# Moving high-part splits to ScalarE, and gate weights and compression weights ahead, in a hybrid decoder layer

## The chip, the cores and the metric

The kernel runs on one core of a Trainium2 chip, as one program. The metric is device microseconds of one execution. The engines are named as in the profile: PE is TensorE's matmuls, PEld its weight loads, DVE is VectorE, ACT is ScalarE, POOL is GpSimd, and SP is the engine that issues nearly all DMAs.

## What is computed

One decoder layer on 512 tokens of width 1024, in float32: a recurrent branch (RG-LRU, width 1344 in four blocks of 336) and native sparse attention (16 heads, 4 key/value groups) share one input projection, are merged by gates, and a squared-ReLU MLP follows. Cut to what the change touches:

```python
xn = rmsnorm(x, norm_mix)
(u_rnn, u_gate, q, k_c, v_c, k_s, v_s, k_w, v_w, g_nsa, g_a, g_b) = jnp.split(xn @ w_in, cuts, axis=-1)
h_a = rg_lru(causal_depthwise_conv(u_rnn, conv_w, conv_b), gate_a_w, gate_a_b, gate_x_w, gate_x_b, lru_lambda)
y_a = h_a * jax.nn.gelu(u_gate, approximate=True)
y_b = nsa_mixer(q, k_c, v_c, k_s, v_s, k_w, v_w, g_nsa, ...)
merged = jax.nn.sigmoid(g_a) * (y_a @ proj_a) + jax.nn.sigmoid(g_b) * (y_b @ proj_b)
h = x + merged @ w_out
return h + jnp.square(jax.nn.relu(rmsnorm(h, norm_mlp) @ w_mlp_in)) @ w_mlp_out
# rg_lru, per block of 336: r, i = sigmoid(block_diag(u)); a = exp(c * r);
# h_t = a_t h_{t-1} + sqrt(1 - a_t^2) (i_t u_t)
# nsa_mixer: rmsnorm over 64 for q, k_s, k_w; k_c, v_c go through compress_blocks (w1, gelu, w2)
```

## The kernel before

**Split precision.** Every matrix product is three matmuls (`mm3`, lines 142 to 144). An operand is cut into a rounded high part (`wh`, line 135 or 137) and a low part, the operand minus its high part (`wl`, line 138, always on VectorE); the product is high times high, high times low, low times high. `split` does this for weights: its flag `act` puts the high part on ScalarE, else it is on POOL. Prepared activations have pairs too: `XH`/`XL` (normed input), `uh`/`ul` (recurrent input, lines 361 and 362), `YH`/`YL` (recurrent output, lines 398 and 399). A tile's first high-times-low matmul can't start before the low part is written, and the low part waits for the high part.

**Order.** The code is written against a tile framework whose scheduler puts the instructions of each engine in one fixed order; `high_priority` pulls splits ahead, `keep_in_program_order` and `issue_after` pin instructions. On the chip each engine runs its list in order and waits where an operand or a buffer is not ready. SP issues the DMAs in such a list too, and stands still where the next one waits.

**Stages, in the profile's microseconds.** Up to 30 the input is normed and transposed. From 30 to 204 stands the recurrent branch: 21 tiles of 128 features (`u_tiles`, 24 matmuls of 512 columns each; tile n has `mm` as its PSUM buffer) and, between them, four recurrent blocks `lru(b)`. A u tile's weights come two tiles at a time (`wraw`, 1 MB, two buffers) and are split (`wh`, `wl`, two buffers each). Its sink is a convolution (`uc`, lines 332 and 334) that a DMA regroups into `ub`, or a gelu (`gs`, `gg`, lines 322 to 325). A block `lru(b)` takes its gate weights (`graw`, two DMAs of 441 KB), splits them (`gwh`, `gwl`), multiplies, and runs a chain over its three parts: tanh (line 375), exp and tanh (376, 377), VectorE's `rr` (379), `ee` = 1 - a (380, POOL), `rr` again (381), `ii` (382), one square root for all three (383), and a scan (387) whose result `y_tile` multiplies by the gelu and splits. The square root and the tanh family need different function tables.

From 204 to 266 four token-major projections of keys and values (`tok_cols`: KS, VS, KW, VW) and the first queries (Q) follow, each in pieces of weights, each with four accumulators of 128 tokens; keys and queries are normed per head (`head_norm`, one tile of 128 tokens at a time, with `rstd_heads`). From 266 to 345 the compression (`ZW` projections, then `phi` with its weights `praw` and `w2r`, split into `pwh`, `pwl`, `w2h`) runs with part of another projection as filler. Then attention to 620, the merge to 725, and the MLP.

The lines the change touches: `split` (126 to 139), `prep` (166), `lru` (356 to 392), `y_tile` (394), `u_tiles` and the calls behind it (400 to 475), `tok_cols` (511), `head_norm` (528), and the sequence of the token-major calls and the compression's loads (617 to 645). The functions follow with the profile's line numbers.

Of the kernel before, what the change touches and what calls it, by code (L numbers as in the profile page):

```python
# [45 lines left out]
GT = 1  # L46
# [23 lines left out]
def layer(ctx, tc, x, norm_mix, w_in, conv_w, conv_b, gate_a_w, gate_a_b, gate_x_w, gate_x_b,  # L70
# [78 lines left out]
    class Cols:  # L149
# [205 lines left out]

    def lru(b):
# [6 lines left out]
        wts = [split(v, 3, BLK, rn, ("gwh", "gwl")) for v in GR.pop(b)]  # L363
# [4 lines left out]
        for j in range(3):  # L368
# [11 lines left out]
            G.tensor_scalar(E[:, j], R[:, j], -1.0, 1.0, op0=OP.mult, op1=OP.add)  # L380
# [13 lines left out]
    def y_tile(t):  # L394
# [80 lines left out]
    for t in (0, 8, 9, 10):  # L475
        y_tile(t)
# [33 lines left out]

    def tok_cols(c0, n, sink):
        step = WH // n
        pss = [psr.tile([128, T], F32, name="lru", bufs=4) for _ in range(4)]
        per = 8 if 8 * n <= WR else 4
        for k0 in [k for c in range(0, 8, per) for k in range(c, c + per, step)]:
            if k0 % per == 0:
                v = raw(128, per, n, (None, rows(win, c0, n)[:, k0:k0 + per]))
            kr = k0 % per
            k1 = min(kr + step, per) - kr + k0
            wh, wl = split(v[:, kr:kr + k1 - k0], k1 - k0, n)  # L520
            for i in range(4):
                ts = slice(128 * i, 128 * i + 128)
                for k in range(k0, k1):
                    mm3(pss[i][:, :n], XH[:, k, ts], XL[:, k, ts], wh[:, k - k0], wl[:, k - k0], k == 0, k == 7)
# [3 lines left out]
    def head_norm(d4, ps, pl):  # L528
# [27 lines left out]
    def q_sink(i, ps):  # L556
        head_norm(QN[0][:, i].rearrange("p (h d) -> p h d", d=64), ps, kvp)
# [59 lines left out]
    with pool("kvp") as kvp:  # L617
# [3 lines left out]
        tok_cols(COL_VW, 304, v_sink(1))  # L621
        for h in range(BC):
            bias_copies(h)
        tok_cols(COL_Q, 256, q_sink)
    with pool("ph") as ph:
# [628 lines left out]
```

## Time and profile before

| what | us |
|---|---|
| runs: median of 3 (lowest to highest) | 1067.66 (1067.63 to 1069.73) |
| the profiled execution, its own time | 1072.21 |
| its span in the trace | 1070.5 |
| PE busy in the span | 1039.5 (97%) |
| DVE, ACT, POOL busy | 664.6, 360.6, 361.4 |

TensorE's mean granted clock in the profiled execution is 0.995. PE is busy in nearly every slice of the span, so what can be won or lost lies in the stretches where it waits or where its clock is lower: the rows below give these one by one. A number in brackets behind an instruction is the idle time just before it on its engine and what ended it.

### The profile page before, as it was taken

The page shows a single profiled execution, that of the slowest core. Times are in us where ns is not written, and L with a number is a line of the kernel's source. Part 1 is how long each engine was busy: PE and PEld are TensorE (multiplying, and loading weights), DVE is VectorE, ACT ScalarE, POOL GpSimd, SP SyncE. Part 2 cuts the span into 40 slices and gives each one's busy share as a digit, 9 for nine tenths or more (in the row PEclk, how much of TensorE's full clock was granted, in tenths as well). Part 3 has the DMA queues.
Part 4 walks back from the last instruction along what each step waited for, and adds up shares of the span by engine and source line. Part 5 has one row for each costly group of instructions (what it writes and reads, how often), then busy time and mean ns, then how long its engine had stood idle before and what let it go on. Part 6 is the DMA issues. An engine that isn't in the chain of part 4 may idle for free.

```text
span 1070.5 us, 14779 instructions
## 1 busy us (share of the span) xinstructions
PE 1039.5 (97%) x5405; PEld 882.1 (82%) x5405; DVE 664.6 (62%) x1227; ACT 360.6 (34%) x770; POOL 361.4 (34%) x397
## 2 busy tenths in 40 slices
PE   6989899999999999999999999999999999999998
PEld 5757676899778898988988888888888888888887
DVE  5579889964675787768778659554333343444443
ACT  4142542522333476756757631032111111111110
POOL 4233344353232464655645433202111121111110
PEclk9989999999999999999999999999999999999999
DMA  7625324243554634424333267512232323322322
GB/s 179 152 83 159 104 75 129 81 125 119 138 156 121 203 93 128 139 81 122 99 122 110 80 226 282 203 46 79 79 118 79 117 80 118 101 97 87 110 79 79
DMA packets 110039, 127.89 MB, mean 119 GB/s; under 512 B 23087, under 2 KB 87375, under 8 KB 109967
## 3 DMA queue, kind: packets, MB, share of 16 engines
q1 hardware_dynamic: 109967, 126.94, 39.2%
q8 instruction: 43, 0.70, 0.3%
q14 instruction: 29, 0.24, 0.1%
HBM read 109.45 MB, written 15.64 MB: 117 GB/s over the span
## 4 chain that ended last, share of the span: by engine, by line
PE 78%; DVE 9%; DMA 6%; issue 4%; POOL 1%; ACT 1%; SPq 0%; DVEq 0%; POOLq 0%; ACTq 0%
PE mf L142 6%; PE mf L143 6%; PE mf L144 6%; PE am L144 5%; PE am L143 5%; PE am L142 5%; PE mi L144 5%; PE mi L142 5%; PE mi L143 5%; PE sc L886 4%; PE po L924 3%; PE pt L905 3%; PE lru L143 3%; PE lru L144 3%; PE lru L142 3%
## 5 line engine op out<-in xcount | busy, mean ns | idle before, releaser
L137 POOL TENSOR_SCALAR wh<-wraw 128x1024 fp32r<-128x1024 f32 (+2 forms) x103 | 110.7, 1075 | 246.5 <-PE mi L143 119.2
L138 DVE TENSOR_TENSOR wl<-wraw,wh 128x1024 fp32r<-128x1024 f32 (+2 forms) x111 | 133.3, 1202 | 54.8 <-POOL wh L137 45.6
L897 POOL TENSOR_SCALAR pp<-pp,sm,gates 128x512 f32<-128x512 f32 (+3 forms) x128 | 93.9, 741 | 67.7 <-DVE sm L895 45.0
L143 PE MATMUL am<-mwl,zh 128*128 128x512 f32 x256 | 99.3, 389 | 0.0
L144 PE MATMUL am<-mwh,zl 128*128 128x512 f32 x256 | 99.3, 389 | 0.0
L142 PE MATMUL am<-mwh,zh 128*128 128x512 f32 x256 | 98.8, 389 | 0.0
L144 PE MATMUL mi<-XH,wl 128*128 128x512 f32 x240 | 93.5, 390 | 0.3 <-DVE wl L138 0.3
L142 PE MATMUL mi<-XH,wh 128*128 128x512 f32 x240 | 93.5, 389 | 0.1
L143 PE MATMUL mi<-XL,wh 128*128 128x512 f32 x240 | 93.4, 389 | 0.0
L1197 DVE TENSOR_TENSOR zl<-Z,zh 128x512 fp32r<-128x512 f32 x32 | 36.3, 1136 | 88.4 <-ACT zh L1196 88.4
L144 PE MATMUL mm<-XH,wl 128*128 128x512 f32 (+1 forms) x216 | 82.4, 383 | 5.5 <-DVE wl L138 5.5
L142 PE MATMUL mm<-XH,wh 128*128 128x512 f32 (+1 forms) x216 | 82.6, 384 | 0.7 <-DVE uc L334 0.6
L143 PE MATMUL mm<-XL,wh 128*128 128x512 f32 (+1 forms) x216 | 82.3, 382 | 1.0 <-DVE XL L225 1.0
L894 ACT ACTIVATE pp<-pp,mx 128x512 f32<-128x512 f32 (+3 forms) x128 | 71.5, 561 | 29.4 <-DVE mx L892 26.6
L1170 DVE SCALAR_TENSOR_TENSOR Z<-mi,zr 128x512 f32<-128x512 f32 x30 | 20.7, 691 | 96.9 <-ACT zr L1169 96.9
L137 POOL TENSOR_SCALAR mwh<-wraw 128x1024 fp32r<-128x1024 f32 x32 | 34.1, 1067 | 138.2 <-PE am L144 131.0
L892 DVE CUSTOM_DVE_ANT_0 pp<-sc,BT 128x512 f32<-128x512 f32 (+3 forms) x128 | 59.0, 484 | 15.1 <-PE pt L905 7.3
L1196 ACT ACTIVATE zh<-Z 128x512 fp32r<-128x512 f32 x32 | 20.3, 633 | 136.5 <-PE am L143 134.4
L1169 ACT ACTIVATE zr<-mi 128x512 f32<-128x512 f32 x30 | 18.0, 600 | 141.7 <-PE mi L144 136.9
L911 ACT ACTIVATE PH<-pt 128x512 fp32r<-128x512 f32 (+1 forms) x96 | 49.3, 524 | 33.9 <-PE pt L905 33.3
L912 DVE TENSOR_TENSOR PL<-pt,PH 128x512 fp32r<-128x512 f32 (+1 forms) x96 | 56.0, 592 | 5.8 <-ACT PH L911 5.6
L886 PE MATMUL sc<-KK,QS 128*128 128x512 f32 (+3 forms) x256 | 57.8, 334 | 0.0
(294 smaller groups left out, 2698.6 us busy)
## 6 DMA issues: line engine op xcount, KB each, us to landing
wraw<-in_w_in_dram SPq DMA_DIRECT2D x26, 1024.0 KB, 5.3
wraw<-in_w_mlp_in_dram SPq DMA_DIRECT2D x16, 1024.0 KB, 5.6
wraw<-in_w_mlp_out_dram SPq DMA_DIRECT2D x16, 1024.0 KB, 4.8
tab_p<-tab_t SPq DMA_DIRECT2D x16, 320.0 KB, 5.0
wraw<-in_proj_a_dram SPq DMA_DIRECT2D x8, 640.0 KB, 5.4
BT<-tab_p SPq DMA_DIRECT2D x16, 256.0 KB, 2.7
wraw<-in_proj_b_dram SPq DMA_DIRECT2D x4, 1024.0 KB, 5.4
wraw<-in_w_out_dram SPq DMA_DIRECT2D x4, 1024.0 KB, 5.6
```

The costliest lines, as they stand in the source:

```text
L137: G.tensor_scalar(h, v, 1.0, 0.0, op0=OP.mult, op1=OP.add)
L138: V.tensor_tensor(l, v, f32(h), op=OP.subtract)
L142: PE.matmul(ps, lh, rh, start=start, stop=False)
L143: PE.matmul(ps, lh, rl, start=False, stop=False)
L144: return PE.matmul(ps, ll, rh, start=False, stop=stop)
L886: ins = PE.matmul(ps[:, cs], grp.Q[r][:, ts], grp.K[br][:, hl, :128 * (i + 1)], start=hl == 0, stop=hl == 1)
L892: V.tensor_tensor_reduce(out=pp[:, cs], in0=ps[:, cs], in1=BTS[h][:, 384 - 128 * i:], scale=1.0, scalar=3e38, op0=OP.add, op1=OP.min, accu ...
L894: S.activation(pp[:, cs], pp[:, cs], AF.Exp, bias=mx, scale=-1.0, accum_out=sm)
L897: G.tensor_scalar(pp[:, cs], pp[:, cs], sm, gt, op0=OP.mult, op1=OP.mult)
L911: S.activation(ph, pv, AF.Copy)
L912: V.tensor_tensor(pl, pv, f32(ph), op=OP.subtract)
L1197: V.tensor_tensor(zl, Z[:, f], f32(zh), op=OP.subtract)
```

## The change

Five edits go together.

1. **Splits on ScalarE.** The high parts of the u tiles 2 to 20 (19 of them) are made by ScalarE, not POOL; the `ee` of the recurrent blocks (12) too, as `Copy` with scale and bias; and the `YH` of the y tiles 1 to 7 (the last call's four stay on POOL). `uh` and `gwh` stay on POOL.
2. **First gate weights early.** `load_gates(0)` is called before the u tiles' sinks, and the gate weights of the first block are split behind the split of tile 5, before `lru(0)` is issued.
3. **Norms of four tiles at once.** `head_norm` copies and squares each of its four tiles and makes the reciprocal roots of all sixteen heads in one go; the query norms of the attention stage keep the old form under the name `row_norm`.
4. **Compression early.** The pool of the compression opens before the token-major calls, and its weights' DMAs and first splits are issued between KW and VW.
5. **Token-major pieces in turn.** VW (304 columns) is loaded as 6 and 2 rows of 128 instead of 4 and 4, in three pieces (3, 3, 2 rows) instead of four (3, 1, 3, 1), and `issue_after` keeps the matmuls of one piece behind those of the piece before.

```diff
-            V.tensor_tensor(l, v, f32(h), op=OP.subtract)
+            split_last[0] = V.tensor_tensor(l, v, f32(h), op=OP.subtract).ins
...
-        def prep(self, n, prio=PRIO):
+        def prep(self, n, prio=PRIO, act=False):
...
+                self.got[n] = split(self.load(n), 8, 128, prio=prio, act=act or self.act, **own)
...
+    def split_gates(b):
+        if b not in GW3:
+            GW3[b] = [split(v, 3, BLK, rn, ("gwh", "gwl")) for v in GR.pop(b)]
...
-        wts = [split(v, 3, BLK, rn, ("gwh", "gwl")) for v in GR.pop(b)]
+        split_gates(b)
+        wts = GW3.pop(b)
         load_gates(b + 1)
...
-            G.tensor_scalar(E[:, j], R[:, j], -1.0, 1.0, op0=OP.mult, op1=OP.add)
+            S.activation(E[:, j], R[:, j], AF.Copy, bias=1.0, scale=-1.0)
...
-        G.tensor_scalar(YH[p:, t], y, 1.0, 0.0, op0=OP.mult, op1=OP.add)
+        if act:
+            S.activation(YH[p:, t], y, AF.Copy)
+        else:
+            G.tensor_scalar(YH[p:, t], y, 1.0, 0.0, op0=OP.mult, op1=OP.add)
...
-            UW.prep(n + 1)
+            UW.prep(n + 1, act=n >= 2)
...
+    load_gates(0)
+    UW.prep(2, act=True)
     for n in range(2):
         u_sink(UO[n])(p2[n])
-    u_tiles(2, 2 + GT)
-    load_gates(0)
-    u_tiles(2 + GT, 6)
+    u_tiles(2, 5)
+    with tc.issue_after(split_last[0]):
+        split_gates(0)
+    u_tiles(5, 6)
...
-        per = 8 if 8 * n <= WR else 4
-        for k0 in [k for c in range(0, 8, per) for k in range(c, c + per, step)]:
+        per = min(8, WR // n // step * step)
+        for k0 in range(0, 8, step):
...
+                if tok_last:
+                    es.enter_context(tc.issue_after(tok_last[-1]))
...
+    def head_norm(d, i, ps, pl, key):
...
+        S.activation(d[:, i], src, AF.Copy)
+        S.activation(SQ[key][:, i], ps[:, :256], AF.Square)
+        if i == 3:
+            rs = rstd_heads(SQ.pop(key).rearrange("p i (h d) -> p (i h) d", d=64), 16, "hrs", pl)
+            rv = rs.rearrange("p (i h) -> p i h", h=4)
+            for n in range(4):
+                V.tensor_tensor(d[:, n], d[:, n], rv[:, n].unsqueeze(2).to_broadcast([128, 4, 64]), op=OP.mult)
...
-    with pool("kvp") as kvp:
+    with pool("ph") as ph:
         tok_cols(COL_KS, 256, k_sink(0))
         tok_cols(COL_VS, 256, v_sink(0))
         tok_cols(COL_KW, 256, k_sink(1))
-        tok_cols(COL_VW, 304, v_sink(1))
-        for h in range(BC):
-            bias_copies(h)
-        tok_cols(COL_Q, 256, q_sink)
-    with pool("ph") as ph:
...
+        tok_cols(COL_VW, 304, v_sink(1))
+        for h in range(BC):
+            bias_copies(h)
+        tok_cols(COL_Q, 256, q_sink)
```

Where it moves instructions, at three places. The first is SP's list at the first u tiles, about 31 to 49 us: the end of the small constants (`pek`, `pev`), the weights of tiles 4 and 5 (`wraw_419`), the regrouping of the convolution (`ub` from `uc`) and the gate weights of the first block (`graw`). Before:

```order
L286 DMA pev_345<-in_phi_v_pe_dram 64x16x1 x2
L122 DMA wraw_419<-in_w_in_dram 128x8x256
L122 DMA wraw_492<-in_w_in_dram 128x8x256
L340 DMA ub_364<-uc_359 112x512
L340 DMA ub_364<-uc_359 16x512
L340 DMA ub_364<-uc_367 96x512
L340 DMA ub_364<-uc_367 32x512
L340 DMA ub_364<-uc_407 80x512
L340 DMA ub_413<-uc_407 48x512
L122 DMA graw_415<-in_gate_a_w_dram 112x3x336
L122 DMA graw_417<-in_gate_x_w_dram 112x3x336
```

and now:

```order
L287 DMA pev_345<-in_phi_v_pe_dram 64x16x1 x2
L121 DMA graw_359<-in_gate_a_w_dram 112x3x336
L121 DMA graw_361<-in_gate_x_w_dram 112x3x336
L121 DMA wraw_419<-in_w_in_dram 128x8x256
L121 DMA wraw_500<-in_w_in_dram 128x8x256
L341 DMA ub_372<-uc_367 112x512
L341 DMA ub_372<-uc_367 16x512
L341 DMA ub_372<-uc_375 96x512
L341 DMA ub_372<-uc_375 32x512
```

Both `graw` loads went from behind the `ub` transfers to just ahead of the weights of tiles 4 and 5.

The second place is POOL at the same tiles: `wh_374`, `wh_378`, `wh_421`, `wh_457`, `wh_494`, `wh_710` are the high parts of the tiles 2 to 7, `gwh` the gate weights' and `uh` the recurrent input's. Before:

```order
L137 TENSOR_SCALAR wh_374<-wraw_284 128x1024
L137 TENSOR_SCALAR wh_378<-wraw_284 128x1024
L137 TENSOR_SCALAR wh_421<-wraw_419 128x1024
L361 TENSOR_SCALAR uh_571<-ub_364 112x512 x2
L137 TENSOR_SCALAR wh_457<-wraw_419 128x1024
L361 TENSOR_SCALAR uh_571<-ub_364 112x512
L455 MEMSET wraw_696 16x128
L460 MEMSET wraw_696 16x16x33
L137 TENSOR_SCALAR gwh_579<-graw_415 112x1008
L137 TENSOR_SCALAR wh_494<-wraw_492 128x1024
L137 TENSOR_SCALAR gwh_583<-graw_417 112x1008
L137 TENSOR_SCALAR wh_710<-wraw_492 128x1024
```

Now POOL has

```order
L138 TENSOR_SCALAR gwh_492<-graw_359 112x1008
L138 TENSOR_SCALAR gwh_496<-graw_361 112x1008
L368 TENSOR_SCALAR uh_579<-ub_372 112x512 x3
L469 MEMSET wraw_696 16x128
L474 MEMSET wraw_696 16x16x33
L368 TENSOR_SCALAR uh_863<-ub_417 112x512
L138 TENSOR_SCALAR gwh_871<-graw_587 112x1008
L138 TENSOR_SCALAR gwh_875<-graw_589 112x1008
```

and the tiles' high parts (`wh_363`, `wh_382`, `wh_421`, `wh_457`) stand on ScalarE among the convolutions' first steps:

```order
L136 ACTIVATE wh_363<-wraw_284 128x1024
L333 ACTIVATE uc_367<-mm_106,cb_311,cw_310 128x512
L136 ACTIVATE wh_382<-wraw_284 128x1024
L333 ACTIVATE uc_375<-mm_107,cb_311,cw_310 128x512
L136 ACTIVATE wh_421<-wraw_419 128x1024
L333 ACTIVATE uc_411<-mm_386,cb_311,cw_310 128x512
L136 ACTIVATE wh_457<-wraw_419 128x1024
```

POOL keeps the gate weights and `uh`, and the gate weights are now first in its list; the tiles' splits went to ScalarE.

The third place is VectorE before tile 10's low part (`wl_1023`), inside the second recurrent block. Before:

```order
L138 TENSOR_TENSOR gwl_1146<-graw_879,gwh_1145 112x1008
L379 SCALAR_TENSOR_TENSOR rr_883<-ee_884,rr_883 112x512
L138 TENSOR_TENSOR gwl_1150<-graw_881,gwh_1149 112x1008
L382 SCALAR_TENSOR_TENSOR ii_885<-ii_885,ub_413 112x512
L381 SCALAR_TENSOR_TENSOR rr_883<-rr_883 112x512
L334 SCALAR_TENSOR_TENSOR uc_1013<-mm_988,cw_310,uc_1013 128x511
L138 TENSOR_TENSOR wl_1023<-wraw_1020,wh_1022 128x1024
L334 SCALAR_TENSOR_TENSOR uc_1013<-mm_988,cw_310,uc_1013 128x510
```

and now:

```order
L139 TENSOR_TENSOR gwl_1146<-graw_879,gwh_1145 112x1008
L387 SCALAR_TENSOR_TENSOR rr_883<-ee_884,rr_883 112x512
L139 TENSOR_TENSOR gwl_1150<-graw_881,gwh_1149 112x1008
L390 SCALAR_TENSOR_TENSOR ii_885<-ii_885,ub_417 112x512
L139 TENSOR_TENSOR wl_1023<-wraw_1020,wh_1022 128x1024
L335 SCALAR_TENSOR_TENSOR uc_1013<-mm_988,cw_310,uc_1013 128x511
L389 SCALAR_TENSOR_TENSOR rr_883<-rr_883 112x512
L335 SCALAR_TENSOR_TENSOR uc_1013<-mm_988,cw_310,uc_1013 128x510
```

Ahead of `wl_1023` the last `rr` of line 381 (now 389) and one step of the convolution went behind it; the two `gwl` and the `ii` stay ahead.

## Rows read from the trace of the kernel before

**Rows 1.** Waits of PE over the span: total us, times, longest us.

```profile
PE mm L144 <- DVE wl L138: 5.5, 4, 3.0
PE lru L144 <- DVE gwl L138: 2.3, 1, 2.3
PE lru L143 <- DVE wl L138: 1.7, 2, 1.5
PE lru L142 <- POOL uh L361: 1.4, 2, 0.9
PE lru L142 <- POOL gwh L137: 1.2, 1, 1.2
...
PE mm L142 <- DVE uc L334: 0.6, 1, 0.6
```

**Rows 2.** Windows: us, busy (count) of PE, PEld, DVE, ACT, POOL, then PEclk, DMA, GB/s.

```profile
130.00:210.00 80.00, 77.72 (x360) 61.82 (x358) 73.01 (x88) 35.77 (x47) 32.13 (x29) 1.00 0.31 94
352.00:620.00 268.00, 268.00 (x1691) 240.45 (x1690) 205.25 (x636) 170.77 (x449) 141.19 (x182) 1.00 0.39 116
```

**Rows 3.** Timeline of PE, tile 4 begins at the second: start us, duration us, instruction.

```profile
40.51 0.39 PE L143 MATMUL mm<-XL,wh 128*128 128x512 f32 x1
...
41.65 0.39 PE L142 MATMUL mm<-XH,wh 128*128 128x512 f32 x1
```

**Rows 4.** Windows with the clock lower, as rows 2.

```profile
57.84:64.00 6.16, 6.16 (x15) 4.43 (x16) 6.16 (x11) 1.76 (x4) 0.86 (x1) 0.50 0.00 0
124.73:129.00 4.27, 4.27 (x12) 3.36 (x13) 4.22 (x8) 0.34 (x1) 0.00 (x0) 0.60 0.00 0
```

**Rows 5.** POOL and VectorE, split of tile 4's weights, timeline.

```profile
38.42 1.05 POOL L137 TENSOR_SCALAR wh<-wraw 128x1024 fp32r<-128x1024 f32 x1 [6.48 <-DMA wraw<-in_w_in_dram]
39.50 1.23 DVE L138 TENSOR_TENSOR wl<-wraw,wh 128x1024 fp32r<-128x1024 f32 x1 [1.53 <-POOL wh L137]
```

**Rows 6.** The window in which those weights land, as rows 2.

```profile
35.00:36.00 1.00, 1.00 (x7) 0.81 (x6) 0.57 (x1) 0.00 (x0) 0.00 (x0) 1.00 1.06 346
```

**Rows 7.** DMA issues between 45 and 60 us: KB each, us to landing.

```profile
graw<-in_gate_a_w_dram SPq DMA_DIRECT2D x1, 441.0 KB, 5.8
```

**Rows 8.** VectorE by form, 20 to 250 us: busy us, mean ns, idle before.

```profile
L138 DVE TENSOR_TENSOR wl<-wraw,wh 128x1024 fp32r<-128x1024 f32 x25 | 30.9, 1236 | 1.8 <-POOL wh L137 1.8
...
L381 DVE SCALAR_TENSOR_TENSOR rr<-rr 112x512 f32<-112x512 f32 x12 | 13.9, 1154 | 5.0 <-POOL ee L380 5.0
...
L138 DVE TENSOR_TENSOR gwl<-graw,gwh 112x1008 fp32r<-112x1008 f32 x8 | 12.2, 1529 | 3.8 <-POOL gwh L137 3.8
```

**Rows 9.** VectorE before tile 10's low part, and POOL beside it, timeline.

```profile
119.31 2.12 DVE L382 SCALAR_TENSOR_TENSOR ii<-ii,ub 112x512 f32<-112x512 f32 x1
121.36 1.52 DVE L381 SCALAR_TENSOR_TENSOR rr<-rr 112x512 f32<-112x512 f32 x1
122.81 0.74 DVE L334 SCALAR_TENSOR_TENSOR uc<-mm,cw,uc 128x511 f32<-128x511 f32 x1
123.47 1.21 DVE L138 TENSOR_TENSOR wl<-wraw,wh 128x1024 fp32r<-128x1024 f32 x1
119.84 2.51 POOL L137 TENSOR_SCALAR wh<-wraw 128x1024 fp32r<-128x1024 f32 x2
```

**Rows 10.** POOL by form, 20 to 250 us.

```profile
L137 POOL TENSOR_SCALAR wh<-wraw 128x1024 fp32r<-128x1024 f32 x25 | 31.9, 1278 | 26.7 <-PE mm L143 15.1 <-DMA wraw<-in_w_in_dram 6.5 <-PE lru L144 3.0
...
L380 POOL TENSOR_SCALAR ee<-rr 112x512 f32<-112x512 f32 x12 | 11.8, 988 | 28.7 <-DVE rr L379 28.7
...
L361 POOL TENSOR_SCALAR uh<-ub 112x512 fp32r<-112x512 f32 x12 | 9.1, 759 | 48.8 <-DMA ub<-uc 30.1 <-PE lru L144 14.8 <-DVE uc L334 3.7
```

**Rows 11.** ScalarE by form, 20 to 350 us.

```profile
L383 ACT ACTIVATE rr<-rr 112x1536 f32<-112x1536 f32 x4 | 6.0, 1491 | 15.1 <-DVE rr L381 15.1
...
L135 ACT ACTIVATE wh<-wraw 128x1024 fp32r<-128x1024 f32 x4 | 4.2, 1059 | 9.2 <-PE lru L144 5.9 <-PE mm L143 3.3
```

**Rows 12.** ScalarE at the compression, timeline.

```profile
280.65 0.31 ACT L661 ACTIVATE w2hk<-w2rk 128x128 fp32r<-128x128 f32 x1 [5.54 <-DMA w2rk<-in_phi_k_w_dram]
```

More of the change, by code (lines that the diff above doesn't have):

```diff
@@ L45 @@
 WK = False
-GT = 1
 PTB = 3
@@ L125, in raw @@
         return v
+    split_last = [None]
     def split(v, a, b, pl=wp, tags=("wh", "wl"), prio=PRIO, bufs=WB, act=False):
@@ L170, in prep @@
                     own = {"pl": self.third, "tags": ("xwh", "xwl"), "bufs": 2}
-                self.got[n] = split(self.load(n), 8, 128, prio=prio, act=self.act, **own)
+                self.got[n] = split(self.load(n), 8, 128, prio=prio, act=act or self.act, **own)
         def get(self, n):
@@ L392, in lru, with y_tile @@
                 SP.dma_start(HY[tb_][pb_:pb_ + c], R[pa_:pa_ + c, j])
-    def y_tile(t):
+    def y_tile(t, act=True):
         p = 64 if t == 0 else 0
@@ L475, in layer @@
     for t in (0, 8, 9, 10):
-        y_tile(t)
+        y_tile(t, False)
     rn_es.close()
@@ L508, in bias_copies @@
             tc.keep_in_program_order(SP.dma_start(tab_p[h], tab_t[h:h + 1].to_broadcast([128, 640])))
+    tok_last = []
     def tok_cols(c0, n, sink):
@@ L513, in tok_cols, with row_norm @@
         pss = [psr.tile([128, T], F32, name="lru", bufs=4) for _ in range(4)]
-        per = 8 if 8 * n <= WR else 4
-        for k0 in [k for c in range(0, 8, per) for k in range(c, c + per, step)]:
+        per = min(8, WR // n // step * step)
+        for k0 in range(0, 8, step):
             if k0 % per == 0:
-                v = raw(128, per, n, (None, rows(win, c0, n)[:, k0:k0 + per]))
+                nk = min(per, 8 - k0)
+                v = raw(128, nk, n, (None, rows(win, c0, n)[:, k0:k0 + nk]))
             kr = k0 % per
-            k1 = min(kr + step, per) - kr + k0
+            k1 = min(k0 + step, 8)
             wh, wl = split(v[:, kr:kr + k1 - k0], k1 - k0, n)
[L521 to L524, printed above, removed]
+            with ExitStack() as es:
+                if tok_last:
+                    es.enter_context(tc.issue_after(tok_last[-1]))
+                for i in range(4):
+                    ts = slice(128 * i, 128 * i + 128)
+                    for k in range(k0, k1):
+                        ins = mm3(pss[i][:, :n], XH[:, k, ts], XL[:, k, ts], wh[:, k - k0], wl[:, k - k0], k == 0, k == 7)
+            tok_last.append(ins.ins)
         for i in range(4):
             sink(i, pss[i])
-    def head_norm(d4, ps, pl):
+    SQ = {}
+    def row_norm(d4, ps, pl):
         sq = pl.tile([128, 4, 64], F32, name="sq", bufs=2)
@@ L534, in head_norm @@
         V.tensor_tensor(d4, d4, rs.unsqueeze(2).to_broadcast([128, 4, 64]), op=OP.mult)
+    def head_norm(d, i, ps, pl, key):
+        if i == 0:
+            SQ[key] = pl.tile([128, 4, T], F32, name="zd" + "kvk"[key])[:, 0:2].rearrange("p a (b c) -> p (a b) c", c=256)
+        src = ps[:, :256].rearrange("p (h d) -> p h d", d=64)
+        S.activation(d[:, i], src, AF.Copy)
[5 more added lines that the diff above has]
+                V.tensor_tensor(d[:, n], d[:, n], rv[:, n].unsqueeze(2).to_broadcast([128, 4, 64]), op=OP.mult)
     def k_sink(br):
         def sink(i, ps):
-            head_norm(kn[:, i, :, br], ps, kvp)
+            head_norm(kn[:, :, :, br], i, ps, ph, br)
         return sink
@@ L556, in q_sink @@
     def q_sink(i, ps):
-        head_norm(QN[0][:, i].rearrange("p (h d) -> p h d", d=64), ps, kvp)
+        head_norm(QN[0].rearrange("p i (h d) -> p i h d", d=64), i, ps, ph, 2)
     def pa_gen():
@@ L762, in q_gen @@
                 if k == 7:
-                    head_norm(QN[g][:, i].rearrange("p (h d) -> p h d", d=64), ps, at)
+                    row_norm(QN[g][:, i].rearrange("p (h d) -> p h d", d=64), ps, at)
                     QN[g, i] = True
```

1 line of the change is left out of this document (added).

## The prediction

> **What bounds the kernel now.** I first read where PE stands still. In attention it never does: 268.00 of 268.00 us [rows 2], and so nothing that the change does there (numbers of buffers, no more) can move the end. What is left lies in the waits of PE [rows 1]. The reader sees six releasers there, five of which are a split that came late: weights' low parts (5.5 and 1.7), gate weights (2.3 and 1.2), `uh` (1.4), and one convolution step (0.6), together 12.7 us. Then I looked behind two of them at the granted clock [rows 4]: after the gate-weight wait that ends at 57.84 the clock is 0.50 of full speed, the lower of its two levels, until 64; after the wait that ends at 124.73 it falls again (mean 0.60). At full clock a matmul of 512 columns follows the last after 0.228 us: five steps from 40.51 to 41.65 [rows 3]. So the 15 matmuls in 6.16 us lost 6.16 - 15 x 0.228 = 2.7, and the 12 in 4.27 lost 4.27 - 12 x 0.228 = 1.5. Waits and slow clock come to 16.9 us, 1.6% of the span: this is all that the change can win at the places it touches. Everything else is PE's own work, which it leaves as it is.
>
> **Who is late, and why.** Between 130 and 210 VectorE is busy 73.0 of 80 us, ScalarE 35.8, POOL 32.1 [rows 2]. VectorE is the full engine, and it is full because its instructions are stretched: the same `rr` of line 381 means 1.15 us over twelve, and the gate weights' low part takes 1.53 although it is smaller than the tiles' low part at 1.24 [rows 8]. Ahead of tile 10's low part stand an `ii` of 2.12 and an `rr` of 1.52, where a step of the convolution, on even more elements, takes 0.74 [rows 9]. In that queue the low part starts at 123.47 and PE goes on at 124.73.
>
> **The change, part by part.**
>
> *First gate weights early.* The wait of 1.2 for `gwh`, that of 2.3 for `gwl` and the slow clock behind it (2.7) hang on `graw`, which is issued behind the `ub` transfers. It now lands before tile 4's weights, its splits stand first in POOL's list, and PE meets the first recurrent matmul inside tile 5, near 48.5, some 8 us after the landing: time for two high parts on an idle POOL and two low parts of 1.53 on VectorE [rows 8] behind tile 5's own. I take all of it: **-6.3** (1.16 + 2.35 + 2.7 unrounded). The two small waits for low parts of the first u tiles, 0.16 and 0.61 (in the 5.5 with four waits: 3.05, 1.71 and these), go with POOL's queue, which mixed these splits with `uh`: **-0.8**.
>
> *What that delays.* The two `graw` loads, 2 x 441 KB [rows 7], now run ahead of tile 4's weights on the same queue. Those landed at 38.42 with 346 GB/s on the way [rows 5, 6]; 0.90 MB more at that rate is 2.6 us, so they land at 41.0. ScalarE's split 1.06 [rows 11], then VectorE's 1.23 [rows 5]: the low part is there at 43.3 to 43.4. PE begins tile 4 at 41.65 [rows 3], 0.16 sooner without the first wait, and wants the low part at its third matmul, 41.95. That is a wait of **+1.4**. Bounds: 0, if the two loads share the engines' idle time before 35 us; and 4.6, if a `graw` costs its own 5.8 from issue to landing (44.2 + 2.3 - 41.95), with a further 2.7 if the clock falls as it did behind 2.3 us of waiting.
>
> *Splits on ScalarE.* POOL loses 19 x 1.28 + 12 x 0.99 = 36 us of the recurrent stretch [rows 10], and seven `YH`; ScalarE gains 19 x 1.06 [rows 11] and 19 half-size ones, half of that each as an estimate, together about 30 us over some 175 us, which at 35.8 of 80 it has. `ee` beside VectorE no longer takes VectorE's time, so the `rr` and `ii` go back towards 0.7, and in front of tile 10's low part one `rr` and a convolution step also went behind it. Of 2.12 + 1.52 + 0.74 [rows 9] one 0.7 remains: 3.7 us sooner, where 3.05 are needed. The waits of this stretch are 3.05 with 1.5 of clock, 1.4 for `uh`, 0.6 for a convolution step and 1.5 for the second piece of KS: 8.05. The margins are thin: late next is the low part of tile 10 itself, which still has two `gwl`s and the new `wh` ahead of it, and the square root, for which ScalarE stands 15.1 us over four blocks [rows 11]; a `wh` behind it in the list now waits too. I keep 1.0 of the 8.05: **-7.0**. Bounds: 0 and 8.05.
>
> *Compression early, pieces in turn, norms together.* The 1.71 belongs to a ZW tile whose split stood behind ScalarE's `w2hk`, which waited 5.54 for its DMA [rows 12]; that DMA is now issued ahead of VW's, and the wait goes. With it goes a piece of Q (1.7 for two waits [rows 1], of which 1.5 was the KS piece): 0.2. Together **-1.9**. The sixteen-wide norms take away nine times three small instructions (reduction, scale, power), and one piece of VW fewer is one split fewer. I cost them at nothing: the next projection's matmuls cover them. Without that cover, PE would wait for a VectorE result as it does for the convolution now, 0.6 [rows 1], in each of three calls. Bounds: a loss of 1.8, and a gain of the 1.9.
>
> **Sum.** -6.3 - 0.8 + 1.4 - 7.0 - 1.9 = **-14.6 us**. Against the profiled execution's 1072.21 that is 1057.6. The median of the runs is 1067.66, 4.55 below it, so I carry the difference over: **1053.1**. With no new wait and nothing kept it is -17.0, 1050.7.
>
> **Rivals.**
>
> *The new load order costs what it saves.* `graw` delays tile 4 by its full landing time, PE waits 4.6 and the clock falls: 4.6 + 2.7 - 1.4 = 5.9 worse, **1059.0**. For it: the weights are the only thing that tile 4 waits on, and POOL had waited 6.48 for them already [rows 5]. Against: the 346 GB/s [rows 6] say that the queue was moving many bytes at once, so the delay is bytes, not latency.
>
> *VectorE stays full.* The eight `gwh` and twelve `uh` stay on POOL. If these, and not `wh` and `ee`, hold up VectorE's instructions, the waits of the recurrent blocks return and 7.0 are lost: **1060.1**. For it: `gwl` is the most stretched kind, and `uh` alone is 9.1 us of POOL [rows 8, 10]. Against: ahead of tile 10's low part the long `ii` and `rr` run beside two `wh` (2.51 from 119.84 [rows 9]), which go.
> The Trainium skill ("SBUF — State Buffer", section "Who interferes with whom") says that a VectorE instruction with two SBUF inputs and a GpSimd instruction that reads SBUF exclude each other for a whole instruction, while ScalarE waits on nobody. By that rule, the trace agrees in 1.53 against 1.24, and every split left on POOL still takes VectorE's time, which is this rival; every one moved gives it back, which is the forecast.
>
> *ScalarE comes late instead (slower).* ScalarE runs in order. A tile's `wh` now stands behind the tanh, exp and `ee` of a block's parts, and `ee` waits for VectorE's `rr`; another stands behind the square root. A tile lasts 24 x 0.228 = 5.5 us and the two halves of a split 1.06 + 1.23, so from the point where ScalarE reaches `wh` over 3.2 us after the buffer came free, PE waits. If that happens once in each of the four blocks at the price seen at tile 10 (3.05 + 1.5), it is 18.2, and the 7.0 are lost too: -14.6 + 7.0 + 18.2 = +10.6, **1078.3**. For it: ScalarE already stands 3.8 us per block before the square root [rows 11]. Against: in most places the new order puts `wh` ahead of that wait, and ScalarE is free for over half the time.
>
> *The edits cancel or do nothing* (the order of waits changes, the same idle time comes back): 1067. The orders of SP, POOL and VectorE above differ at the very places where PE waits, so this is small.
>
> **Chances.** Forecast 0.62; load order 0.13; VectorE full 0.15; ScalarE late 0.07; cancelling 0.03. The predicted time is the forecast's. The range takes in the first two rivals and the best case: 1050.7 less some 1.7, since single runs of this kernel lie up to 2.1 us apart, gives 1049.0, and 1060.1 with 1.4 for the same reason 1061.5. A measurement of this kernel can tell about 0.2%, 2.1 us, from no change. The first three cases are all faster by more: 0.90; cancelling 0.03; slower 0.07.
>
> **What would show it.** Right: no wait for `gwh` or `gwl` before the first recurrent matmul, and a granted clock of 1.00 from 54 to 64 us; a wait near 42 us of 1 to 2 us for tile 4's split, put down to the DMA or to ScalarE; line 389's `rr` near 0.7 us; no wait of over 1 us between 110 and 215; none for `w2hk`. Wrong: a clock of 0.50 near 45 us (first rival); `rr` and `ii` still above 1.1 (second); waits of PE for a low part whose `wh` ScalarE made late, once per block (third). A profiled span above 1068 would refute the sum.

## The result, and the profile after

The changed kernel takes **1059.24 us** (median of 4 runs, 1058.78 to 1059.99), against 1068.70 for the kernel before in the same comparison (4 runs): a ratio of 0.9912, 95% interval 0.9895 to 0.9929. It is 9.5 us faster; 1053.1 was forecast, and the range, 1049.0 to 1061.5, holds it. The profiled execution took 1059.58 with a span of 1057.9, 12.6 us less than before's.

The waits of PE over the span, as in [rows 1], now read:

```profile
...
PE lru L143 <- DVE VV L582: 4.8, 1, 4.8
PE mm L143 <- ACT wh L136: 1.8, 1, 1.8
...
PE lru L144 <- DVE wl L139: 0.6, 1, 0.6
...
PE mm L145 <- DVE wl L139: 0.5, 1, 0.5
```

Of the six releasers of [rows 1], those for gate weights, `uh` and the convolution are gone, and so are the long waits for low parts. There are two new places: tile 4 (1.8 and 0.5) and one wait of 4.8 us for `VV`, a releaser that [rows 1] does not have at all. Both as PE's timeline shows them:

```profile
43.13 0.50 PE L143 MATMUL mm<-XH,wh 128*128 128x512 f32 x1 [1.78 <-ACT wh L136]
...
44.39 0.50 PE L145 MATMUL mm<-XH,wl 128*128 128x512 f32 x1 [0.53 <-DVE wl L139]
...
218.35 0.55 PE L143 MATMUL lru<-wh,XH 128*128 128x256 f32 x1 [4.82 <-DVE VV L582]
```

Behind the wait that ends at 218.35 the clock is at the lower level; where it was before, from 57 to 64, it is full (windows: us, busy and count by engine, PEclk, DMA share, GB/s):

```profile
218.35:224.30 5.95, 5.95 (x28) 5.95 (x29) 4.66 (x8) 0.00 (x0) 0.00 (x0) 0.50 0.61 138
57.00:64.00 7.00, 7.00 (x32) 5.30 (x31) 4.33 (x11) 4.41 (x8) 0.00 (x0) 1.00 0.57 164
```

At full clock a 256-column matmul follows the last after 0.12 us (seen behind 225 us), so 28 in 5.95 us lost 5.95 - 28 x 0.12 = 2.6.

Where the time went can be read from the starts of three stages: the first matmul of KS, of VW (304 columns) and of the transposed keys. Before:

```profile
203.52 0.64 PE L142 MATMUL lru<-wh,XH 128*128 128x256 f32 x4
...
239.86 0.30 PE L142 MATMUL lru<-wh,XH 128*128 128x304 f32 x1
...
352.06 0.60 PE L790 MATMUL pt<-ident,kn 128*128 128x128 f32 x4
```

and after:

```profile
189.50 0.64 PE L143 MATMUL lru<-wh,XH 128*128 128x256 f32 x4
...
232.60 0.30 PE L143 MATMUL lru<-wh,XH 128*128 128x304 f32 x1
...
340.74 0.60 PE L826 MATMUL pt<-ident,kn 128*128 128x128 f32 x4
```

KS begins 14.0 us sooner, but VW only 7.3: between them KS, VS and KW gave back 6.8. By the keys the lead is 11.3 (the compression's waits went), and at the end of the span 12.6.

What stands behind the 4.8 is in two lists. VectorE, at KS's norm and VS's accumulators:

```profile
211.96 4.78 DVE L571 TENSOR_TENSOR kn<-kn,hrs 128x256 f32<-128x256 f32 x4 [3.03 <-POOL hrs L517]
216.66 1.21 DVE L139 TENSOR_TENSOR wl<-wraw,wh 128x1024 fp32r<-128x1024 f32 x1
217.80 0.41 DVE L582 TENSOR_TENSOR VV<-lru,VV 128x256 fp32r<-128x256 f32 x1
```

and POOL beside it:

```profile
209.01 2.92 POOL L517 TENSOR_TENSOR hrs<-hrs,halfs 128x16 f32<-128x16 f32 x1 [2.20 <-DVE hrs L516]
211.90 1.05 POOL L138 TENSOR_SCALAR wh<-wraw 128x1024 fp32r<-128x1024 f32 x1
212.91 2.39 POOL L138 TENSOR_SCALAR pwh<-praw 128x1024 fp32r<-128x1024 f32 x2
```

The power for sixteen heads takes 2.92 us on POOL. VectorE waits 3.03 for it with the four multiplies of the norm, which then take 4.78 beside POOL's splits of KW's and the compression's weights; KW's low part stands behind them, and behind that the first subtraction of VS. Until that is done at 218.2 VS's accumulator is not free, and KW's first matmul wants it. KW's own high part, too, stands behind the power in POOL's list.

### The profile page after: what moved, and what is told of

It reads as the page before. It is cut to its first block, busy times and chain, and to the rows that moved or that the text cites. A ratio compares the mean times of both kernels' runs of the same rounds, so it can differ in the third digit from the quotient of the medians.

```text
span 1057.9 us, 14717 instructions
## 1 busy us (share of the span) xinstructions
PE 1033.8 (98%) x5405; PEld 882.6 (83%) x5405; DVE 647.4 (61%) x1208; ACT 388.6 (37%) x808; POOL 310.3 (29%) x349
## 4 chain that ended last, share of the span: by engine, by line
PE 90%; DVE 3%; DMA 2%; ACT 2%; issue 2%; POOL 1%; SPq 0%; DVEq 0%; ACTq 0%; POOLq 0%
PE mf L143 6%; PE mf L144 6%; PE mf L145 6%; PE am L145 5%; PE am L144 5%; PE am L143 5%; PE mi L145 5%; PE mi L143 5%; PE mi L144 5%; PE sc L922 4%; PE po L960 4%; PE pt L941 3%; PE mm L144 3%; PE mm L145 3%; PE mm L143 3%; PE lru L143 3%
## 5 line engine op out<-in xcount | busy, mean ns | idle before, releaser
L138 POOL TENSOR_SCALAR wh<-wraw 128x1024 fp32r<-128x1024 f32 (+3 forms) x83 | 85.7, 1033 | 250.4 <-PE mi L144 119.1
```

## The experiments

Each is the changed kernel with one edit, unless said otherwise; times are to be read against its 1059.24, and each ratio, to the kernel before, against its 0.9912 (0.9895 to 0.9929). Only the intervals of runs 6, 8, 9 and 12 lie apart from that one; in the others the waits in the traces decide, not the time. Two theories on the new wait: **N**, the sixteen-wide norm is in the way; **P**, the compression's early splits are.

**1. The old norms back.**

```diff
-            head_norm(kn[:, :, :, br], i, ps, ph, br)
+            row_norm(kn[:, i, :, br], ps, ph)
-        head_norm(QN[0].rearrange("p i (h d) -> p i h d", d=64), i, ps, ph, 2)
+        row_norm(QN[0][:, i].rearrange("p (h d) -> p h d", d=64), ps, ph)
```

> The changed kernel with the old key and query norms, one tile of 128 tokens at a time; all else as changed (median 1059.24). Theory N (the sixteen-wide norm is what stands in VectorE's way): its four multiplies wait 3.03 us for one power of 2.92 us on POOL and hold up the subtractions of VS, whose accumulators KW needs. With the old norms the wait of 4.8 us at KW's first matmul falls below 1 us, and the half clock behind it goes: 1052.7 (1051 to 1054.5). Theory P (the compression's early splits are in the way, on POOL and on VectorE): four powers of about 1.08 take longer than one of 2.92, the splits stand where they stood, and the wait stays at 4 to 5 us: 1059 (1058 to 1061).

Measured: 1060.33 (1056.97 to 1063.59), ratio 0.9915 (0.9891 to 0.9938): nothing gained. But P's reason was wrong too: the `VV` wait is gone, and another of almost the same size stands 8 us earlier.

```profile
PE lru L143 <- ACT sq L556: 4.3, 1, 4.3
PE mm L143 <- ACT wh L136: 2.7, 1, 2.7
```

ScalarE holds KS's accumulators, since its squares wait for one of two small buffers that VectorE's sum has not read yet: VectorE is still at the `YL` of the last y tiles and a low part. The lower clock follows there as well (0.50 from 210.06 to 216.00). So the batched norm cured one wait of this size and made another.

**2. The compression's low parts behind VS's subtractions** (on VectorE alone; the first of three such places).

```diff
-        w1p = {parts[0]: split(..., ("pwh", "pwl"), prio=0)}
+        with tc.issue_after(vv_last[3]):
+            w1p = {parts[0]: split(..., ("pwh", "pwl"), prio=0)}
```

> The changed kernel with VectorE's low parts of the compression's weights (two of 1.21 us, two of 0.28) put behind the four subtractions of VS instead of between them; POOL's list as changed. Theory P: the four low parts, 3.0 us, are taken out of the path of the accumulators; the wait at KW falls from 4.8 to about 2 us: 1056 (1054.5 to 1057.5). Theory N: the first subtraction, which ends the wait, stands ahead of the low parts already; the wait stays 4.8 and the half clock too: 1059 (1058 to 1060.5).

Measured: 1059.66, ratio 0.9909 (0.9889 to 0.9928), and the wait is 4.8 to the digit. P's part on VectorE falls; its part on POOL is not touched here.

**3. Tile 4's weights ahead of the gate weights.**

```diff
+    UW.load(4)
     load_gates(0)
```

> The changed kernel with the load of the weights of tiles 4 and 5 issued ahead of the first gate weights, not behind them. If the two waits at tile 4 (1.78 and 0.53) are the price of the gate weights' 0.9 MB ahead of it, both go and no new wait appears at the first recurrent matmul near 50 us, since it comes some 8 us after the gate weights would land: 1056.5 (1055.5 to 1058). Rival: the gate weights now land as late as tile 4's weights did and their splits meet tile 5's, so that the wait moves to the first recurrent matmul: 1059 (1058 to 1061).

Measured: 1062.33, ratio 0.9929 (0.9907 to 0.9950), no gain. Tile 4's waits are gone, and the rival's kind of wait is there, dearer than expected and at another instruction:

```profile
50.22 0.77 PE L143 MATMUL mm<-XH,wh 128*128 128x512 f32 x1 [3.21 <-DVE uc L335]
```

VectorE's list has the low part of `uh` ahead of the convolution's last step, and that low part waits for a regrouping transfer, which lands only near 47:

```profile
47.73 1.69 DVE L369 TENSOR_TENSOR ul<-ub,uh 112x512 fp32r<-112x512 f32 x2 [4.66 <-POOL uh L368]
49.34 0.73 DVE L335 SCALAR_TENSOR_TENSOR uc<-mm,cw,uc 128x509 f32<-128x509 f32 x1
```

So tile 4's wait had covered a second lateness, that of the regrouping transfers issued behind these loads (in the change POOL gets the first of them at 46.4).

**4. The norm's multiplies behind VS's subtractions.** The sixteen-wide norm stays.

```diff
+            def scale():
                 for n in range(4):
                     V.tensor_tensor(d[:, n], d[:, n], ...)
+            if key == 0: LATER.append(scale)
...
+            if i == 3 and LATER:
+                with tc.issue_after(last.ins):
+                    LATER.pop()()
```

> The changed kernel with the sixteen-wide norm, but the four multiplies of KS put behind the four subtractions of VS in VectorE's list; the compression's low parts stay between the subtractions. Theory N: the multiplies' wait and their 4.78 us leave the path; the first subtraction then waits only for KW's low part, whose high part POOL finishes near 213, so PE waits about 1 us at KW and the clock stays: 1053 (1051.5 to 1055). Theory P: what held the subtractions was POOL's and VectorE's work for the compression, so the wait stays above 3 us: 1058 (1057 to 1060).

Measured: **1056.31**, ratio 0.9881 (0.9860 to 0.9901). N holds, short of its size: the wait falls from 4.8 to 2.0, not to 1, because KW's high part still follows the power on POOL (it ends at 213.3) and its low part, beside the compression's splits, takes 2.05 instead of 1.21:

```profile
213.30 2.05 DVE L139 TENSOR_TENSOR wl<-wraw,wh 128x1024 fp32r<-128x1024 f32 x1 [4.06 <-POOL wh L138]
215.27 0.41 DVE L588 TENSOR_TENSOR VV<-lru,VV 128x256 fp32r<-128x256 f32 x1
...
220.29 1.41 DVE L573 TENSOR_TENSOR kn<-kn,hrs 128x256 f32<-128x256 f32 x4
```

The last line shows something else. Where POOL is idle the four multiplies take 1.41, not 4.78; the 3.4 between is about what POOL's three splits beside them took in the change (1.05 and 2.39). So P's splits on POOL can lengthen the wait, by up to 2.4 as an estimate from these numbers, but only by way of the norm's multiplies: run 8 settles this.

**5. The load for tiles 6 and 7 held back.**

```diff
+            if n == 5:
+                with tc.issue_after(HOLD):
+                    UW.load(6)
```

`HOLD` is the last regrouping transfer of tiles 0 and 1.

> The changed kernel with the load of the weights of tiles 6 and 7 held behind the regrouping transfers of tiles 0 and 1; the gate weights and tile 4's weights stay where the change puts them. Theory B (tile 4's wait is bytes: gate weights, two loads of 1 MB and the regrouping transfers share some 340 GB/s from 34 to 42 us, and half of what runs beside tile 4's weights is the load for tiles 6 and 7): tile 4's weights land near 40 instead of 42.0, and of the waits of 1.78 and 0.53 at most 0.6 are left: 1057 (1056 to 1058.5). Rival (order, not bytes: the gate weights alone stand ahead, and what comes behind does not matter): no change, 1059 (1058 to 1060.5).

Measured: 1061.56, ratio 0.9933 (0.9919 to 0.9948). A miss for both: tile 4's weights landed later (ScalarE's split began at 43.22, not 42.02) and the wait grew to 3.6. Taking that load off the bytes beside tile 4's did not bring them forward. In this execution SP also reached the loads 0.7 us later, so the true cost of the hold stays open.

**6 and 7. The u tiles' high parts, and the step 1 - a, back on POOL.**

```diff
-            UW.prep(n + 1, act=n >= 2)
+            UW.prep(n + 1)
```

> The changed kernel with the high parts of the u tiles back on POOL; the step 1 - a and the first y tiles stay on ScalarE. Theory S (VectorE's instructions were stretched by POOL's splits of weights beside them): the splits come back beside them, the rr, ii and gwl groups are longer again, and waits of PE return in the recurrent blocks and at tile 4 or 5: 1064 (1061.5 to 1068). Rival (the step 1 - a alone, which sat in VectorE's own chain, was what delayed it): 1059 (1058 to 1061).

```diff
-            S.activation(E[:, j], R[:, j], AF.Copy, bias=1.0, scale=-1.0)
+            G.tensor_scalar(E[:, j], R[:, j], -1.0, 1.0, op0=OP.mult, op1=OP.add)
```

> The changed kernel with the twelve steps 1 - a back on POOL; the weights' splits stay on ScalarE. Theory S: POOL has little else left there, the twelve instructions cost VectorE some 0.3 us each and the chain one more hop, and nothing at PE: 1059.5 (1058 to 1062). Rival (the chain's hop over POOL was what delayed VectorE): waits of the recurrent blocks return, 1064 (1062 to 1067).

Measured: **1078.45**, ratio 1.0091 (1.0074 to 1.0108), and 1061.77, ratio 0.9938 (0.9922 to 0.9954). The first is 19 us slower than the change, beyond what S expected, for a reason besides S: the gate weights' splits now stand ahead of the tiles' in POOL's list and wait for their load, so that PE stands 9.6 us at the start of the u tiles:

```profile
40.30 0.79 PE L143 MATMUL mm<-XH,wh 128*128 128x512 f32 x1 [9.60 <-POOL wh L138]
...
180.53 0.77 PE L143 MATMUL lru<-uh,gwh 112*112 112x512 f32 x1 [4.00 <-POOL uh L368]
```

In the recurrent blocks S shows: the wait of 4.0 for `uh`, three below 1 (0.27, 0.73, 0.91), and VectorE's groups stretched. The 19 us divide into about 11 at the start (9.60 and 0.85 of waits against the change's 1.78 and 0.53, and 3.1 of clock: 47 matmuls in 13.85 us up to 55, at full clock 0.228 each) and about 7.5 in the blocks (5.9 of waits, and 1.6 of clock behind the 4.00: 8 matmuls in 3.47 us). From 50 to 210 us, the change (first) and the splits on POOL (second):

```profile
L139 DVE TENSOR_TENSOR gwl<-graw,gwh 112x1008 fp32r<-112x1008 f32 x8 | 9.7, 1227 | 0.9 <-POOL gwh L138 0.9
...
L389 DVE SCALAR_TENSOR_TENSOR rr<-rr 112x512 f32<-112x512 f32 x12 | 8.5, 718 | 0.4 <-ACT ee L388 0.3
L369 DVE TENSOR_TENSOR ul<-ub,uh 112x512 fp32r<-112x512 f32 x10 | 7.6, 758 | 1.9 <-POOL uh L368 1.9
```

```profile
L369 DVE TENSOR_TENSOR ul<-ub,uh 112x512 fp32r<-112x512 f32 x11 | 11.5, 1048 | 3.7 <-POOL uh L368 3.7
...
L389 DVE SCALAR_TENSOR_TENSOR rr<-rr 112x512 f32<-112x512 f32 x12 | 10.8, 908 | 0.1
...
L139 DVE TENSOR_TENSOR gwl<-graw,gwh 112x1008 fp32r<-112x1008 f32 x8 | 10.8, 1353 | 0.0
```

And one `uh` there, from the timelines of POOL and VectorE:

```profile
175.49 4.98 POOL L368 TENSOR_SCALAR uh<-ub 112x512 fp32r<-112x512 f32 x1 [6.27 <-DMA ub<-uc]
```

```profile
175.48 1.21 DVE L139 TENSOR_TENSOR wl<-wraw,wh 128x1024 fp32r<-128x1024 f32 x1
176.61 3.44 DVE L395 TENSOR_TENSOR_SCAN rr<-ee,ii 112x512 f32<-112x512 f32 x3
180.51 1.52 DVE L369 TENSOR_TENSOR ul<-ub,uh 112x512 fp32r<-112x512 f32 x1 [0.46 <-POOL uh L368]
```

It ends at 180.47, when VectorE's low part and three scans are over (180.05); another `uh` in the same list, at 167.57, takes 0.63.

The step 1 - a alone costs little: two new waits of 0.4 and 0.7, and one grown from 0.6 to 0.8, while its `rr` means 940 ns. Its median is 2.5 above the change's, inside what S gave and not clear of noise.

**8. Norm's tail and compression's low parts behind VS, with the hold of run 5.** The whole tail of KS's norm, the power too, goes into `LATER`.

> The changed kernel with three moves: the whole tail of KS's norm (sum, power, multiplies) behind VS's subtractions, the compression's low parts behind them too, and the load for tiles 6 and 7 held as in the run on that alone. Theory N with B: PE's wait at KW falls below 0.5 us and the half clock behind it goes (7.4 us of waiting and clock), tile 4's waits fall by 1.7: 1059.2 - 7 - 1.7 = 1050.5 (1049 to 1053). If the late norm now holds up a projection behind it (VW's or Q's first piece waits for a low part or for POOL's power), a wait of 1 to 3 us comes back there: 1053 (1051.5 to 1055).

Measured: **1053.86**, ratio 0.9864 (0.9847 to 0.9880). The wait at KW is gone with the power out of POOL's way, though the compression's splits stand on POOL as before, and VS's first subtraction begins beside them at 210.62:

```profile
210.05 1.52 POOL L138 TENSOR_SCALAR pwh<-praw 128x1024 fp32r<-128x1024 f32 x1 [0.65 <-DMA praw<-in_phi_k_w_dram]
```

With run 2, in which the low parts alone gained nothing, this leaves N as the cause. Tile 4's wait is 2.1, with a clock of 0.53 behind it.

**9. The first gate weights late again.**

```diff
-    load_gates(0)
     UW.prep(2, act=True)
...
-    u_tiles(2, 5)
-    with tc.issue_after(split_last[0]):
-        split_gates(0)
-    u_tiles(5, 6)
+    u_tiles(2, 3)
+    load_gates(0)
+    u_tiles(3, 6)
```

> The changed kernel with the first gate weights loaded and split where the kernel before had them, behind the regrouping transfers; all other edits stay. Theory G (the waits for them hang on when they are loaded): the load lands near 54 us again, PE waits for both halves (about 3.5 us) with a half clock behind it (2.7), and tile 4's waits (1.78 and 0.53) go: 1059.2 + 6.5 - 2.8 = 1063 (1061.5 to 1065). Rival (POOL's mixed list was what made them late, and that list is now free): only tile 4's waits change, 1057 (1055.5 to 1058.5).

Measured: 1064.58, ratio 0.9963 (0.9949 to 0.9977): G's time, in part by another road. The gate weights' waits come back as 1.07, 0.52 and 0.53, with a full clock, and in the second block `uh` comes 3.76 late, with a mean clock of 0.69 behind it to 97.2:

```profile
54.04 0.49 PE L143 MATMUL lru<-uh,gwh 112*112 112x512 f32 x1 [1.07 <-POOL gwh L138]
...
93.74 0.95 PE L143 MATMUL lru<-uh,gwh 112*112 112x512 f32 x3 [3.76 <-POOL uh L368]
```

**10. Without the pins that keep the pieces in turn.**

```diff
-                if tok_last:
+                if False:
```

> The changed kernel without the pins that keep one piece's matmuls behind those of the piece before (VW's three pieces stay). On TensorE alone some matmuls of VS and KW change places within a piece. Theory N: the wait at KW comes from VectorE's list, which is the same: 1059 (1058 to 1061). Theory T (held in turn, PE stands before accumulators that are not free while it could have gone on): the wait at KW shrinks by 1 us or more, 1057 (1055 to 1058).

Measured: 1057.35, ratio 0.9894 (0.9876 to 0.9912). The time is T's, the reason is not: PE waits as long as in the change, in two parts (3.5 for the second piece of VS, whose first matmuls moved up in TensorE's list and came there before their split was made, then 1.1 and 0.2 for `VV`). In the profiled execution the clock stays full behind both (windows as above):

```profile
205.44:212.00 6.56, 6.56 (x53) 6.50 (x54) 3.49 (x5) 0.34 (x1) 4.37 (x3) 1.00 1.11 243
217.02:224.00 6.98, 6.75 (x53) 6.41 (x54) 5.17 (x8) 0.00 (x0) 0.43 (x1) 1.00 0.60 134
```

That is not where its 2 us come from, though: its four executions had mean clocks of 1.000, 0.996, 0.998 and 0.997 and took 1057.88, 1056.61, 1056.82 and 1058.51, so the one with the full clock is not the shortest. What the turn costs stays open.

**11 and 12. The loads ahead of the small constants, alone and with run 8's two moves behind VS.** In the changed kernel SP issues the constants one by one up to 32.4 us and only then the gate weights:

```profile
23.57 1.34 SPq L276 DMA_DIRECT2D qg<-in_q_norm_dram  x2
...
30.74 1.66 SPq L287 DMA_DIRECT2D pev<-in_phi_v_pe_dram  x2
32.44 0.66 SPq L121 DMA_DIRECT2D graw<-in_gate_a_w_dram  x1
```

```diff
+    UW.prep(2, act=True)
     load_gates(0)
-    UW.prep(2, act=True)
+    UW.load(4)
...
+    with tc.issue_after(raw_last[0].ins):
+        qg0 = dup_col(q_norm[0].rearrange("(d o) -> d o", o=1), "qg0")
...
```

> The changed kernel with the weights of tiles 4 and 5 and the first gate weights loaded ahead of the last small constants (six and more tiny transfers that SP issues between 24 and 32 us), so that tile 4's weights are issued near 24 us and the gate weights near 28. Theory I (tile 4 is late since its load is issued late, behind SP's small transfers, and then shares the bytes): the weights land before 32, both waits at tile 4 go, nothing takes their place: 1056.5 (1055.5 to 1058). Rival: as when the gate weights went behind, VectorE's list meets the regrouping transfers at tile 5 or 6 and PE waits there instead, with a half clock: 1060 (1058.5 to 1063).

> Two moves on the changed kernel: the load order of the run on the constants, and the norm's tail and the compression's low parts behind VS's subtractions as in the combined run (without its hold, which gained nothing). If the two gains add: 1053.9 of the combined run less tile 4's wait of 2.13, the 0.3 around it and the half clock behind it (1.4): 1050 (1048.5 to 1052). If tile 4's wait only moves: 1053.5 (1052 to 1056).

Measured: **1056.98**, ratio 0.9894 (0.9877 to 0.9911), and **1049.65** (1049.49 to 1050.09), ratio **0.9823** (0.9809 to 0.9838). Both as forecast. Tile 4's load is issued at 23.6, ahead of the twelve constants that the edit moves, and the first gate weights' between 28 and 31, in the midst of them; ScalarE splits tile 4's at 36.4 and 36.1, and PE does not wait for it. The regrouping transfers come sooner too: run 11's first `uh` starts at 43.5, run 3's, with the same order of weights behind the constants, at 47.1. In the last kernel, the best of all, PE's waits behind 28 us and before attention are 0.5, 0.8 and 0.6 (PE's timeline; the wait for `hg` is one of before and of the change too):

```profile
204.85 0.39 PE L146 MATMUL lru<-wl,XH 128*128 128x256 f32 x1 [0.48 <-DVE wl L141]
...
291.06 0.44 PE L749 MATMUL lru<-ident,hg 128*128 128x128 f32 x2 [0.82 <-DVE hg L311]
...
321.79 0.47 PE L145 MATMUL mf<-YH,wh 128*128 128x512 f32 x1 [0.56 <-ACT spl L287]
```

## Why the prediction held, and was 6 us too low

Of the 6 us about 2 come from the sum and about 4 from carrying it over to the median. That the range held is in part luck. Its upper end stands on the rivals at 1059.0 and 1060.1, and neither is what happened: tile 4 waits 2.3 us with the clock full, and the recurrent blocks have no waits. What did happen, 7.4 us between KS and KW, lay outside the bounds of its own term.

**First gate weights early (-6.3): right.** No wait for `gwh` or `gwl` is left and the clock is full from 57 to 64. The two small waits (0.8) are gone as well. Run 9 gives the whole edit its price, 5.3 us with what it costs at tile 4, though most of the waiting that comes back is for `uh`.

**What that delays (+1.4): right in kind, 0.9 too small.** The weights landed at 42.0, not 41.0. The step left out that SP issued them later (at 33.71, in the kernel before at 32.26) and that the regrouping transfers ran beside them too; which of these made the difference no run shows. The half clock of the first rival did not follow in the change, though it did in runs 1, 5 and 8 behind waits there of 2.7, 3.6 and 2.1. Run 3 shows that the wait hangs on the order of the two loads, and runs 11 and 12 that it was no need: with the loads issued among SP's small transfers, not behind them, nothing takes its place.

**Splits on ScalarE (-7.0): right, and all of it came.** None of the waits of the recurrent blocks is left, nor that of KS's second piece (the 0.6 for `wl` in the list above is VS's second piece, at 207.64). Run 6 puts about 7.5 on the blocks when these splits go back. `rr` means 0.72 where it meant 1.15, `gwl` 1.23 where it meant 1.53 [rows 8]. The rival that VectorE stays full falls: what remained on POOL did not stretch it enough to matter, as run 6 shows by putting the rest back. The rival that ScalarE comes late falls too; no wait in the blocks names it. The rule of the Trainium skill ("SBUF — State Buffer", section "Who interferes with whom"), that a VectorE instruction with two SBUF inputs and a GpSimd one that reads SBUF keep each other waiting, stands here: in run 6 the `uh` of 4.98 us lasted as long as VectorE's four instructions of two SBUF inputs beside it, and 0.63 in another place. Run 4's 1.41 against 4.78 says the same of VectorE; both are better signs than the prediction's 1.53 against 1.24, since both of those kinds have two SBUF inputs.

**Norms together (nothing): this step failed.** The prediction said that the next projection's matmuls cover them, and put the price without that cover at 0.6 in each call. What measured 4.8 of wait and 2.6 of clock was one call, KS's. The prediction compared counts of instructions and not one chain: sum, power on POOL, multiplies, with two lists standing still behind them. Its cover ended where the accumulators ran out: four of them, held by VS until VectorE came to it. Run 4 takes part of it back, runs 8 and 12 all. The width of sixteen is not the whole cause: with the old norms (run 1) PE waits 4.3 there, 8 us earlier, since VectorE is still at the last y tiles when KS, now 14 us sooner, wants it. The compression's splits on POOL make it longer where the norm's multiplies run beside them (run 4), but are no cause of their own (run 8). So the cover failed for a norm of KS of either width.

**Compression early (-1.9): right** for the waits that it names, and the 0.6 for `pwl` went as well. That its early splits on POOL would stretch KS's norm it left out.

**The sum.** Against the profiled execution -14.6 was forecast and -12.6 measured, but by stages, from the leads above, the two differ more:

| us won | forecast | measured |
|---|---|---|
| up to KS's first matmul | 11.2 | 14.0 |
| KS to VW | 1.5 | -6.8 |
| VW to the transposed keys | 1.9 | 4.1 |
| behind | 0 | 1.3 |

(11.2 is 6.3 + 0.8 - 1.4, and of the 7.0 all but KS's 1.5.) So an error of 8 between KS and VW is hidden by 6 won elsewhere. Most of what was won there has a reason in the old trace, too: a wait costs more than its number, so that the 16.9 us of listed waits and clock were not all that could be won. PE's timeline of before around tile 10's wait:

```profile
121.29 0.40 PE L143 MATMUL mm<-XL,wh 128*128 128x512 f32 x1
124.73 0.50 PE L144 MATMUL mm<-XH,wl 128*128 128x512 f32 x1 [3.05 <-DVE wl L138]
125.06 0.40 PE L142 MATMUL mm<-XH,wh 128*128 128x512 f32 x1
```

From 121.29 to 125.06 are two steps, 0.46 at full pace; 3.3 are lost, where 3.05 is listed. Eight such waits vanished before KS (0.16, 0.61, 1.16, 2.35, 3.05, two for `uh`, one for the convolution), so this term is about 2, and the 1.0 that the forecast kept back came as well; at tile 4 0.9 and, for two new waits, 0.5 go the other way, and about 1 of the 14.0 stays open. From VW on, four waits vanished (0.25, 0.22, 1.71 and 0.62 for `pwl`, 2.8 together), with some 0.27 around each 3.9 of the 4.1. The 1.3 behind are two waits of before (0.38 at 621.66 and 0.35 at 692.64, so counted about 1.3) that this execution of the change does not have; waits at these two places come and go between the runs above, so this is hardly the change's.

**The carrying over: this step failed too,** by 4.2 us. Before's profiled execution stood 4.55 above the median of its runs, the changed one's 0.34 above its own. The forecast carried the 4.55 over in full, as if it had nothing to do with what is removed. But the lower clock does not fall in every execution. The profiled one of before has a mean clock of 0.995. Of twelve later executions of before on one chip the one at 0.995 took 1071.34, and the eight at 0.998 took 1066.92 to 1069.09; in run 1, one kernel took 1063.59 at 0.993 and 1056.97 at 0.998. The 4.2 us of slow clock in [rows 4] are thus in part a loss of that execution, which the median had not in full and the change could not win back from it. This is read from the times and clocks of whole executions; no run shows it place by place.

With no new wait and nothing kept the prediction had 1050.7; the best kernel, run 12, takes 1049.65, and its four executions have clocks of 0.999 and 1.000. So much could be had by two moves more on the changed kernel.

## What to carry to other kernels

When an engine's list is in order, price a step that is batched by its longest chain and by who stands behind it in every list it crosses, not by the instructions saved; then ask which buffer of the consumer runs out first. And before a load is reordered against its neighbours, look at when the queue first reaches any of them: here twelve tiny transfers held SP for 8.8 us (23.57 to 32.40) ahead of all these loads.

## What the runs showed of the hardware

The lower clock does not follow from the length of one wait. At tile 4 it fell behind 2.1 us (run 8), and not behind 2.3 with 0.5 soon after (run 2), nor behind 1.8 and 0.5 in the change; at KW it fell behind 2.0 (run 4); in VS it stayed full behind 3.5 (run 10). The windows behind these waits, of run 8, run 2 and run 4:

```profile
43.65:47.00 3.35, 3.35 (x8) 2.59 (x9) 3.35 (x4) 2.23 (x3) 1.57 (x2) 0.53 0.87 269
```

```profile
44.50:49.00 4.50, 4.50 (x21) 3.69 (x21) 3.40 (x5) 0.83 (x2) 1.24 (x2) 1.00 0.28 68
```

```profile
216.00:220.00 4.00, 4.00 (x22) 3.83 (x22) 4.00 (x7) 0.00 (x0) 2.23 (x2) 0.62 0.28 79
```

Run 8's window lost 3.35 - 8 x 0.228 = 1.5 on top of the 2.1, run 4's 4.00 - 22 x 0.12 = 1.4 on top of 2.0, run 2's nothing. So a wait of 2 us costs here about its length or 1.7 times that, and the mean clock of one kernel's executions differs too (0.993 to 0.998 in run 1): a reason to remove it rather than to shorten it.
